# The causal mask of stick-breaking attention: from products on TensorE into VectorE's running sum

## The chip, the cores and the metric

The kernel runs on one core of one Trainium2 chip. The metric is the device time of one execution in microseconds; lower is better. The engines are named as the profile names them: PE is TensorE's matmul and PEld its weight load, DVE is VectorE, ACT is ScalarE, POOL is GpSimd, SP is SyncE, which issues most loads.

## The reference

One transformer block over 16 learned meta tokens and 512 tokens of width 1024: RMSNorm, one input projection for two attention branches of eight heads each, projections, gates, and a SwiGLU. The change lies in the first branch, stick-breaking attention:

```
z = jnp.einsum('bhqd,bhkd->bhqk', q, k).astype(jnp.float32) * (SB_HEAD_DIM ** -0.5)
causal = kpos[None, :] < qpos[:, None]
u = jnp.where(causal, jax.nn.log_sigmoid(-z), 0.0)
rest = lax.cumsum(u, axis=3, reverse=True) - u
log_a = jax.nn.log_sigmoid(z) + rest
a = jnp.where(causal, jnp.exp(log_a), 0.0)
return jnp.einsum('bhqk,bhkd->bhqd', a.astype(v.dtype), v)
```

A query sees only keys in front of it. With softplus(z) = max(z, 0) + ln(1 + exp(-|z|)), log_a is z minus the sum of softplus(z) over the visible keys from this one to the last visible one. The sum therefore runs from the last key back.

## The kernel before

Weights are split into a high and a low part (`split`, L78 on ACT, L79 on DVE), and each product is made of three matmuls (`mm3`, L290 to L292). Loads go through a ring of staging tiles from SP. Sums of weights for a seven-product scheme are made by accumulating DMAs that POOL issues (`tick`, L145), a few after each unit of work.

The main loop goes over eight stick-breaking heads and then eight differential heads. While a head's attention runs, PE does the projections of the next head ("units") between its stages: a head is a generator that yields how many units come before its next stage. The start of the program, up to the projections of head 0, is written in a fixed order for PE, DVE and ACT; from there a scheduler orders each engine's instructions by priority. In head 0 four further units (`sum_units`, L496 to L513) make sums of the activations (`f_t`, `tA`, `tB`) on DVE and ACT.

A stick-breaking head (`sb_head`) goes through these stages:

- Scores. Four blocks of 128 queries meet all keys up to their own (256, 272, 416 columns, and 528 in two halves). They lie in two PSUM tiles of two banks: `zA` holds blocks 0 to 2, `zB` block 3. Behind each block's three matmuls one more (L620) adds the mask: `ident_b`, a 128x128 identity in bfloat16, times `mask_b`, which holds -1e30 where key >= query and 0 elsewhere. It covers the 128 columns at the block's diagonal (144 for block 2).
- ACT takes Abs, Exp, Ln (L632 to L634), DVE makes softplus in `s` (L635).
- DVE sums `s` from the last key back, in place, with one scan per block (L639).
- DVE subtracts from the scores (L640), ACT takes the exponential (L641).
- `attn_out` transposes the weights on PE (L556, L568, L571), ACT and DVE split them (`a_h` L558, `a_l` L559), PE multiplies by the values (`vh`, `vl`, `vf`), and L659/L660 store the result. The values were transposed and split in `turn` (L532 to L540).

A masked score of about -1e30 has softplus 0, adds nothing to the sum, and its exponential is 0.

`mask_b` is made on POOL at the start (L1000, L1001), `ident_b` on DVE (L1004). A differential head makes a 128x528 table `bias` from `dist` on POOL (L700), in a single buffer of the pool `att`; DVE reads it with the scores (L711).

Of the kernel before, what the change touches and what calls it, by code (L numbers as in the profile page):

```python
# [9 lines left out]
F32 = mybir.dt.float32  # L10
F32R = mybir.dt.float32r
BF16 = mybir.dt.bfloat16
AF = mybir.ActivationFunctionType
ALU = mybir.AluOpType
AX = mybir.AxisListType

P = 128
D = 1024
SEQ = 512
NM = 16  # L20
L = NM + SEQ
KT = D // P
HL = L // 2
# [9 lines left out]
BIG = 1.0e30  # L33
# [8 lines left out]
def block_kernel(ctx: ExitStack, tc: tile.TileContext, x, meta, norm_mix_g, w_in, w_gate, b_gate,  # L42
                 lam_q1, lam_k1, lam_q2, lam_k2, subln_g, w_br_sb, w_br_df, w_out, norm_ffn_g,
                 w_ffn_gate, w_ffn_up, w_ffn_down, norm_final_g, out):
    nc = tc.nc
# [5 lines left out]
    const = ctx.enter_context(tc.tile_pool(name="const", bufs=1))  # L51
# [12 lines left out]
    def z_tile():  # L64
        return ps_z.tile([P, 2, 512], F32, tag="z", name="z")
# [221 lines left out]
    def mm3(ps, pairs, start=True, stop=True, skip=False):  # L287
        n = len(pairs)
        for i, (ah, al, bh, bl) in enumerate(pairs):
            nc.tensor.matmul(ps, lhsT=ah, rhs=bh, start=(start and i == 0), stop=False, skip_group_check=skip)  # L290
            nc.tensor.matmul(ps, lhsT=ah, rhs=bl, start=False, stop=False, skip_group_check=skip)  # L291
            nc.tensor.matmul(ps, lhsT=al, rhs=bh, start=False, stop=(stop and i == n - 1), skip_group_check=skip)  # L292
# [66 lines left out]
    ident = const.tile([P, P], F32, name="ident")  # L359
    make_identity(nc, ident)  # L360

    mask_b = const.tile([P, 144], BF16, name="mask_b")

    dist = const.tile([P, L], F32, name="dist")
    ident_b = const.tile([P, P], BF16, name="ident_b")
    ones_r = const.tile([P, P], F32R, name="ones_r")
    eps_t = const.tile([P, 1], F32, name="eps_t")
    pcol = const.tile([P, 33], F32, name="pcol")
# [27 lines left out]
    ap_ = att.enter_context(tc.tile_pool(name="att", bufs=1))  # L396
# [6 lines left out]

    a_s = ap_.tile([P, 256], F32, name="a_s")
    nc.gpsimd.memset(a_s, 0.0)

    def kv_units(key, evac):
        def unit(hf):
            s = slice(hf * HL, (hf + 1) * HL)
            ps = mm_tile()  # L410
            proj(ps[:, 0:HL], weights(key), xT, s)
            with tc.high_priority(offset=EVAC):
                evac(ps[:, 0:HL], s)

        return [lambda: unit(0), lambda: unit(1)]
# [195 lines left out]
    def sb_head(h, d, o_h, o_l):  # L611
        qh, ql = d["q"]
        kh, kl = d["k"]
        zA, zB = z_tile(), z_tile()

        def score(o, t, k0, k1, mo, mn):
            q = slice(t * P, (t + 1) * P)
            mm3(o, [(qh[:, q], ql[:, q], kh[:, k0:k1], kl[:, k0:k1])], stop=(mn == 0))
            if mn:
                nc.tensor.matmul(o[:, mo:mo + mn], lhsT=ident_b, rhs=mask_b[:, 0:mn], start=False, stop=True)  # L620

        score(zA[:, 0, 0:256], 0, 0, 256, NM, P)
        score(zA[:, 0, 144:416], 1, 0, 272, NM + P, P)
        score(zA[:, 1, 0:416], 2, 0, 416, NM + 2 * P, 144)
        score(zB[:, 0, 0:HL], 3, 0, HL, 0, 0)
        score(zB[:, 1, 0:HL], 3, HL, L, 400 - HL, P)
        res = []
        for z, n in ((zA, 416), (zB, HL)):
            zz = z[:, :, 0:n]
            e = ap_.tile([P, 2, n], F32, tag=("w2" if n == 416 else "w1"), name="e")  # L630
            s = ap_.tile([P, 2, n], F32, tag=("w3" if n == 416 else "w0"), name="s")
            nc.scalar.activation(e, zz, AF.Abs)  # L632
            nc.scalar.activation(e, e, AF.Exp, scale=-1.0)
            nc.scalar.activation(e, e, AF.Ln, bias=1.0)  # L634
            nc.vector.scalar_tensor_tensor(s, zz, 0.0, e, op0=ALU.max, op1=ALU.add)  # L635
            sf = s.rearrange("p a b -> p (a b)")
            for a, b in (((0, 144), (144, 416), (416, 832)) if n == 416 else ((0, L),)):
                f = sf[:, a:b][:, ::-1]
                nc.vector.tensor_tensor_scan(f, f, f, 0.0, op0=ALU.add, op1=ALU.bypass)  # L639
            nc.vector.tensor_tensor(s, zz, s, op=ALU.subtract)  # L640
            nc.scalar.activation(s, s, AF.Exp)  # L641
            res.append(sf)
        base = ((0, 0), (0, 144), (0, 416), (1, 0))
        zs = []

        def banks():
            if zs:
                return [z[:, 1] for z in zs]
            zs.extend((z_tile(), z_tile()))
            return [z[:, 0] for z in zs]  # L650

        t1, t2, av = attn_out(lambda t, k0, k1: res[base[t][0]][:, base[t][1] + k0:base[t][1] + k1], d, 96, banks)
        yield 4 if h + 1 < SEVEN else 5
        t1()
        yield 1
        t2()
        yield 1
        ps = av()
        nc.scalar.copy(o_h, ps)  # L659
        nc.vector.tensor_tensor(o_l, ps, o_h.bitcast(F32), op=ALU.subtract)  # L660
# [291 lines left out]
    zA, zB = z_tile(), z_tile()  # L952
# [33 lines left out]
    for k in range(KT):  # L986
# [10 lines left out]
    pm = mm_tile()  # L997
    nc.tensor.transpose(pm[:, 0:33], prow, ident[0:33, 0:33])
    nc.vector.tensor_copy(pcol[:, 8:33], pm[:, 8:33])
    nc.gpsimd.memset(mask_b, 0.0)  # L1000
    nc.gpsimd.affine_select(out=mask_b, in_=mask_b, pattern=[[-1, 144]], compare_op=ALU.is_gt,  # L1001
                            fill=-BIG, base=0, channel_multiplier=1)
    nc.vector.tensor_copy(ones_r, onesf)
    nc.vector.tensor_copy(ident_b, ident)  # L1004
    order.close()
    units[5]()
    turn()
    todo = []
    for br in range(2):
        name, head = (("y_sb", sb_head), ("y_df", df_head))[br]  # L1010
        if br:
            nc.gpsimd.memset(a_s, 0.0)
            y_out.append(xtp.tile([P, KT, SEQ], F32, tag="y_sb", name="y_out"))
        for h in range(NH):
# [5 lines left out]
            if h % 2 == 0:  # L1020
                o = [opool.tile([P, 2, SEQ], F32R, tag=t, name=t) for t in ("o_h", "o_l")]
# [513 lines left out]
```

## Time and profile before

| | |
|---|---|
| median of 3 runs | 954.66 us (953.51 to 954.71) |
| the profiled execution's own time | 955.27 us |
| its span | 953.5 us |
| mean granted TensorE clock | 0.998 |
| DMA, mean over the span | 166 GB/s |
| 32 mask products on PE (L620) | 230 ns each by the profile |
| 32 scans on DVE (L639) | 25.1 us busy |

The span runs from the first to the last instruction; the execution's own time has 1.8 us around it. Rows of the timeline give start, duration, engine, line, operation and what it writes and reads, then in brackets the idle time before it and what ended it. A PE row lasts until its result is out, and the next one starts long before that, so distances between starts tell what a matmul costs. The stick-breaking heads fill about 22 to 254 us, the differential heads the time to about 500 us.

### The profile page before, as it was taken

The page shows a single profiled execution, that of the slowest core. Times are in us where ns is not written, and L with a number is a line of the kernel's source. Part 1 is how long each engine was busy: PE and PEld are TensorE (multiplying, and loading weights), DVE is VectorE, ACT ScalarE, POOL GpSimd, SP SyncE. Part 2 cuts the span into 40 slices and gives each one's busy share as a digit, 9 for nine tenths or more (in the row PEclk, how much of TensorE's full clock was granted, in tenths as well). Part 3 has the DMA queues.
Part 4 walks back from the last instruction along what each step waited for, and adds up shares of the span by engine and source line. Part 5 has one row for each costly group of instructions (what it writes and reads, how often), then busy time and mean ns, then how long its engine had stood idle before and what let it go on. Part 6 is the DMA issues. An engine that isn't in the chain of part 4 may idle for free.

```text
span 953.5 us, 16249 instructions
## 1 busy us (share of the span) xinstructions
PE 940.6 (99%) x6105; PEld 851.1 (89%) x6106; DVE 720.8 (76%) x1336; ACT 592.8 (62%) x1137; POOL 190.5 (20%) x212
## 2 busy tenths in 40 slices
PE   8999999999999999999999999999999999999996
PEld 5988989898999899998987888899999999988886
DVE  7978777765677666876662578899888888989875
ACT  7765676666566666666676356765555555666654
POOL 3200121222133343344513530001000000000013
PEclk9999999999999999999999999999999999999999
DMA  8525678778777879799987865527743343276642
GB/s 246 154 63 149 164 176 204 159 166 228 198 178 174 213 170 185 181 204 180 199 198 168 260 197 170 150 78 171 155 123 111 90 120 103 67 255 203 198 151 89
DMA packets 155824, 158.42 MB, mean 166 GB/s; under 512 B 6465, under 2 KB 117218, under 8 KB 155746
## 3 DMA queue, kind: packets, MB, share of 16 engines
q1 hardware_dynamic: 132690, 101.61, 35.5%
q0 software_dynamic: 22896, 55.72, 28.6%
q8 instruction: 48, 0.79, 0.3%
q14 instruction: 30, 0.25, 0.1%
q10 hardware_dynamic: 160, 0.07, 0.0%
HBM read 133.64 MB, written 50.86 MB: 193 GB/s over the span
## 4 chain that ended last, share of the span: by engine, by line
PE 90%; DVE 6%; ACT 2%; issue 1%; DMA 1%; ACTq 0%; DVEq 0%
PE mm L290 21%; PE mm L291 21%; PE mm L292 21%; PE z L290 6%; PE z L291 6%; PE z L292 6%; PE z L708 1%; PE z L707 1%; DVE wl L79 1%; PE tr L556 1%; PE tr L532 1%; PE z L556 1%; DMA slots<-in_w_ffn_down_dram 1%; PE z L584 1%; DVE hres L1212 1%
## 5 line engine op out<-in xcount | busy, mean ns | idle before, releaser
L290 PE MATMUL mm<-xT_h,wh 128*128 128x264 f32 (+2 forms) x656 | 214.5, 327 | 0.5 <-ACT xT_h L912 0.5
L291 PE MATMUL mm<-xT_l,wh 128*128 128x264 f32 (+2 forms) x656 | 213.4, 325 | 0.5
L292 PE MATMUL mm<-xT_h,wl 128*128 128x264 f32 (+2 forms) x656 | 212.5, 324 | 0.0
L79 DVE TENSOR_TENSOR wl<-wst,wh 128x1024 fp32r<-128x1024 f32 (+1 forms) x147 | 164.2, 1120 | 44.9 <-ACT wh L78 44.7
L78 ACT CAST wh<-wst 128x1024 fp32r<-128x1024 f32 (+1 forms) x147 | 141.6, 965 | 84.7 <-PE mm L291 62.5
L291 PEld LDWEIGHTS mm<-xT_l,wh 128*128 128x128 f32 x656 | 123.5, 188 | 10.1 <-DVE xT_l L913 1.3
L290 PEld LDWEIGHTS mm<-xT_h,wh 128*128 128x128 f32 x656 | 123.5, 188 | 10.0 <-ACT xT_h L912 0.9
L292 PEld LDWEIGHTS mm<-xT_h,wl 128*128 128x128 f32 x656 | 123.4, 188 | 10.0
L290 PE MATMUL mm<-hT_h,wh 128*128 128x256 f32 x304 | 85.7, 284 | 0.4 <-ACT hT_h L1169 0.4
L292 PE MATMUL mm<-hT_h,wl 128*128 128x256 f32 x304 | 86.0, 284 | 0.0
L291 PE MATMUL mm<-hT_l,wh 128*128 128x256 f32 x304 | 86.0, 283 | 0.0
L290 PEld LDWEIGHTS mm<-hT_h,wh 128*128 128x128 f32 x304 | 57.3, 189 | 0.6 <-ACT hT_h L1169 0.6
L291 PEld LDWEIGHTS mm<-hT_l,wh 128*128 128x128 f32 x304 | 57.6, 190 | 0.0
L292 PEld LDWEIGHTS mm<-hT_h,wl 128*128 128x128 f32 x304 | 57.4, 189 | 0.0
L711 DVE CUSTOM_DVE_ANT_0 pr<-z,bias 128x144 f32<-128x144 f32 (+3 forms) x64 | 30.9, 501 | 35.0 <-PE z L708 34.9
L290 PE MATMUL mm<-o_h,wh 128*128 128x512 f32 x128 | 53.2, 416 | 0.0
L1437 POOL TENSOR_TENSOR outs<-hres,gF 128x512 f32<-128x512 f32 x4 | 6.2, 1554 | 226.0 <-DVE hres L1423 217.8
L291 PE MATMUL z<-wl,da 128*128 128x512 f32 (+1 forms) x132 | 50.4, 381 | 0.3 <-DVE wl L79 0.3
L145 POOL DMA_DIRECT2D ds<-in_w_ffn_down_dram x36 | 30.1, 840 | 102.3 <-ACT wh L78 68.6
L291 PE MATMUL mm<-o_l,wh 128*128 128x512 f32 x128 | 50.1, 392 | 0.3 <-DVE o_l L779 0.3
L290 PE MATMUL z<-wh,da 128*128 128x512 f32 (+1 forms) x132 | 50.2, 381 | 0.0
L292 PE MATMUL z<-wh,da 128*128 128x512 f32 (+1 forms) x132 | 50.2, 380 | 0.0
(375 smaller groups left out, 2554.4 us busy)
## 6 DMA issues: line engine op xcount, KB each, us to landing
wst<-in_w_in_dram SPq DMA_DIRECT2D x40, 512.0 KB, 5.7
ds<-in_w_ffn_down_dram POOLq DMA_DIRECT2D x30, 512.0 KB, 6.2
wst<-in_w_ffn_gate_dram SPq DMA_DIRECT2D x22, 512.0 KB, 4.0
wsu<-in_w_ffn_up_dram SPq DMA_DIRECT2D x20, 512.0 KB, 3.8
wst<-in_w_gate_dram SPq DMA_DIRECT2D x16, 512.0 KB, 6.8
y_df<-y_out POOLq DMA_DIRECT2D x32, 256.0 KB, 7.4
slots<-ds SPq DMA_DIRECT2D x13, 512.0 KB, 3.4
os<-in_w_out_dram POOLq DMA_DIRECT2D x12, 512.0 KB, 5.4
```

The source lines that it names most:

```text
L78: cast["last"] = (hi_copy or nc.scalar.copy)(hi, src)
L79: (lo_eng or nc.vector).tensor_tensor(lo, src, hi.bitcast(F32), op=ALU.subtract)
L145: tc.add_manual_dep(nc.gpsimd.dma_start(dst, src, **kw).ins, cast["last"].ins.name, paced)
L290: nc.tensor.matmul(ps, lhsT=ah, rhs=bh, start=(start and i == 0), stop=False, skip_group_check=skip)
L291: nc.tensor.matmul(ps, lhsT=ah, rhs=bl, start=False, stop=False, skip_group_check=skip)
L292: nc.tensor.matmul(ps, lhsT=al, rhs=bh, start=False, stop=(stop and i == n - 1), skip_group_check=skip)
L532: nc.tensor.transpose(pt[:, j * P:(j + 1) * P], vT[:, j * P:(j + 1) * P], ident)
L556: nc.tensor.transpose(pt[:, (t - j) * P:(t - j + 1) * P], blocks(t, j * P, (j + 1) * P), ident)
L584: nc.tensor.matmul(ps.rearrange("p (t q) -> p t q", q=P)[:, :, lo_rows:P], lhsT=vf[:, 1], rhs=a_s[:, 0:4 * qn], start=False, stop=True)
L707: nc.tensor.matmul(o, lhsT=q[c][:, qs], rhs=k[c][:, 0, k0:k1], start=True, stop=False)
L708: nc.tensor.matmul(o, lhsT=q[c][:, qs], rhs=k[c][:, 1, k0:k1], start=False, stop=True)
L711: nc.vector.tensor_tensor_reduce(po, zz, bb, scale=1.0, scalar=-3.0e38, op0=ALU.add, op1=ALU.max, accum_out=mx[:, t, c:c + 1])
```

## The change

The mask leaves the scores. Each scan now computes state = `resets` x state + `s`, from the last key back, and begins at 1e30. Over the keys behind the last visible one the state stays at about 1e30 (their softplus is lost in it), so their weights become exp(-1e30) = 0. `resets` is 1 except at one key per query, the last visible one, where it is 0: there the state falls to that key's own softplus, and the sum runs on from there. The table is 528 wide: ones, set by POOL, and 1 minus the identity in columns 399 to 526, made by DVE. A block of n columns reads the last n columns of it. It lies in the buffer that `bias` uses later (the pool `att` has one such buffer).

```
-    mask_b = const.tile([P, 144], BF16, name="mask_b")
-    ident_b = const.tile([P, P], BF16, name="ident_b")
+    resets = ap_.tile([P, L], F32, tag="bias", name="resets")
...
-        def score(o, t, k0, k1, mo, mn):
+        def score(o, t, k0, k1):
             q = slice(t * P, (t + 1) * P)
-            mm3(o, [(qh[:, q], ql[:, q], kh[:, k0:k1], kl[:, k0:k1])], stop=(mn == 0))
-            if mn:
-                nc.tensor.matmul(o[:, mo:mo + mn], lhsT=ident_b, rhs=mask_b[:, 0:mn], start=False, stop=True)
+            mm3(o, [(qh[:, q], ql[:, q], kh[:, k0:k1], kl[:, k0:k1])])
...
-            for a, b in (((0, 144), (144, 416), (416, 832)) if n == 416 else ((0, L),)):
+            for a, b in (((0, 144), (144, 416), (416, 816)) if n == 416 else ((0, L),)):
                 f = sf[:, a:b][:, ::-1]
-                nc.vector.tensor_tensor_scan(f, f, f, 0.0, op0=ALU.add, op1=ALU.bypass)
+                nc.vector.tensor_tensor_scan(f, resets[:, L - (b - a):][:, ::-1], f, BIG, op0=ALU.mult, op1=ALU.add)
...
-    nc.gpsimd.memset(mask_b, 0.0)
-    nc.gpsimd.affine_select(out=mask_b, in_=mask_b, pattern=[[-1, 144]], compare_op=ALU.is_gt,
-                            fill=-BIG, base=0, channel_multiplier=1)
+    nc.gpsimd.memset(resets, 1.0)
+    nc.vector.tensor_scalar(resets[:, 399:399 + P], ident, -1.0, 1.0, op0=ALU.mult, op1=ALU.add)
     nc.vector.tensor_copy(ones_r, onesf)
-    nc.vector.tensor_copy(ident_b, ident)
```

On PE, in the scores of head 1, this stands before (from the second block's last product on):

```order
L292 MATMUL z<-kh,ql 128x272
L620 LDWEIGHTS ident_b
L620 MATMUL z<-mask_b,ident_b 128x128
L290 MATMUL z<-kh,qh 128x416
L291 MATMUL z<-kl,qh 128x416
L292 MATMUL z<-kh,ql 128x416
L620 LDWEIGHTS ident_b
L620 MATMUL z<-mask_b,ident_b 128x144
L290 MATMUL z<-kh,qh 128x264
```

and this now (lines below the first edits are 3 to 5 lower in the changed kernel):

```order
L292 MATMUL z<-kh,ql 128x272
L290 MATMUL z<-kh,qh 128x416
L291 MATMUL z<-kl,qh 128x416
L292 MATMUL z<-kh,ql 128x416
L290 MATMUL z<-kh,qh 128x264
```

Four weight loads and four matmuls are gone from each head; in heads 1 to 7 nothing else on PE is moved. On DVE, in head 0, this stood between the last sum tile of the first two steps (`tB`) and the subtractions (the scans are shown as scalar_tensor_tensor on `s` alone):

```order
L501 SCALAR_TENSOR_TENSOR tB<-f_t_591,tB 128x528
L535 TENSOR_TENSOR vl<-tr,vh 128x384
L79 TENSOR_TENSOR wl<-wst,wh 128x1024
L496 TENSOR_TENSOR f_t_592<-xT_h,xT_l 128x528
L635 SCALAR_TENSOR_TENSOR s<-z,e 128x832
L496 TENSOR_TENSOR f_t_594<-xT_h,xT_l 128x528
L639 SCALAR_TENSOR_TENSOR s<-s 128x144
L639 SCALAR_TENSOR_TENSOR s<-s 128x272
L639 SCALAR_TENSOR_TENSOR s<-s 128x416
L635 SCALAR_TENSOR_TENSOR s<-z,e 128x528
L640 TENSOR_TENSOR s<-z,s 128x832
L639 SCALAR_TENSOR_TENSOR s<-s 128x528
```

and this stands there now:

```order
L534 TENSOR_TENSOR vl<-tr,vh 128x384
L500 SCALAR_TENSOR_TENSOR tB<-f_t_587,tB 128x528
L79 TENSOR_TENSOR wl<-wst,wh 128x1024
L495 TENSOR_TENSOR f_t_588<-xT_h,xT_l 128x528
L495 TENSOR_TENSOR f_t_590<-xT_h,xT_l 128x528
L632 SCALAR_TENSOR_TENSOR s<-z,e 128x832
L632 SCALAR_TENSOR_TENSOR s<-z,e 128x528
L636 SCALAR_TENSOR_TENSOR s<-resets,s 128x144
L636 SCALAR_TENSOR_TENSOR s<-resets,s 128x272
L636 SCALAR_TENSOR_TENSOR s<-resets,s 128x400
L636 SCALAR_TENSOR_TENSOR s<-resets,s 128x528
L637 TENSOR_TENSOR s<-z,s 128x832
```

`vl` and `tB` have changed places, the second `f_t` is ahead of the softplus steps, both softplus steps are ahead of the scans, and all four scans are ahead of the first subtraction. ACT's order moves with it in head 0: `vh` is cast before the small copy `v_s`, and Abs of the 528-column scores comes before Ln of the 832-column ones. On PE, in head 0 alone, the last two transposes of the second score turn (L556) stand two matmuls later, the third turn two, and the product with the values one.

On POOL the table of the first differential head stood near the start (`os` and `ds` are DMAs of the weight sums):

```order
L922 TENSOR_TENSOR wl<-wst,wh 128x1024
L996 MEMSET dist 64x64
L700 TENSOR_SCALAR bias<-dist 128x528
L145 DMA os_2_77<-in_w_out_dram 256x1x512
L145 DMA os_0_78<-in_w_out_dram 256x1x512
```

and stands now at the change of branches, in front of the DMAs that copy the keys of that head (`dk`):

```order
L145 DMA ds_8_94<-in_w_ffn_down_dram 256x1x512
L800 DMA y_sb_117<-ys 128x512
L697 TENSOR_SCALAR bias<-dist 128x528
L145 DMA ds_10_95<-in_w_ffn_down_dram 128x512
L687 DMA dk_2785<-dk_2785 64x1056
L687 DMA dk_2786<-dk_2786 64x1056
```

It waits there until the last scan of stick-breaking head 7 has read `resets`.

More of the change, by code (lines that the diff above doesn't have):

```diff
@@ L614, in sb_head @@
         zA, zB = z_tile(), z_tile()
-        def score(o, t, k0, k1, mo, mn):
+        def score(o, t, k0, k1):
             q = slice(t * P, (t + 1) * P)
-            mm3(o, [(qh[:, q], ql[:, q], kh[:, k0:k1], kl[:, k0:k1])], stop=(mn == 0))
-            if mn:
[L620 to L626, printed above, removed]
+            mm3(o, [(qh[:, q], ql[:, q], kh[:, k0:k1], kl[:, k0:k1])])
+        score(zA[:, 0, 0:256], 0, 0, 256)
+        score(zA[:, 0, 144:416], 1, 0, 272)
+        score(zA[:, 1, 0:416], 2, 0, 416)
+        score(zB[:, 0, 0:HL], 3, 0, HL)
+        score(zB[:, 1, 0:HL], 3, HL, L)
         res = []
```

## The prediction

> **What bounds the kernel now.** I read the page's busy line and its chain of work first, then the busy times by stage (each row of the windows: stretch, its length, then busy time and count of PE, PEld, DVE, ACT, POOL, the granted clock, the DMA share).
>
> ```profile
> PE 940.6 (99%) x6105; PEld 851.1 (89%) x6106; DVE 720.8 (76%) x1336; ACT 592.8 (62%) x1137; POOL 190.5 (20%) x212
> PE 90%; DVE 6%; ACT 2%; issue 1%; DMA 1%; ACTq 0%; DVEq 0%
> 22.00:57.00 35.00, 34.13 (x256) 32.08 (x256) 34.89 (x60) 23.93 (x47) 8.14 (x5) 1.00 0.38 106
> 85.00:113.00 28.00, 28.00 (x187) 25.13 (x184) 20.53 (x32) 17.17 (x33) 3.81 (x5) 1.00 0.56 149
> 197.00:225.00 28.00, 28.00 (x184) 25.17 (x185) 18.63 (x29) 18.55 (x36) 6.48 (x9) 1.00 0.73 157
> ```
>
> The chain is 90% PE. But a share over the whole run says little about this change, which touches only the eight stick-breaking heads. There the windows show two regimes. In heads 1 to 7 PE is busy 28.00 of 28.00 us at clock 1.00 while DVE has about 20 of 28. In head 0 (22 to 57 us) DVE is the full engine, 34.89 of 35.00. The chain of waits in order of time confirms it: one row per head for the score transposes, always at the same distance.
>
> ```profile
> 80.72 0.76 PE z L556 x7
> 108.68 0.77 PE z L556 x7
> ...
> 249.81 0.77 PE z L556 x7
> ```
>
> 108.68 − 80.72 = 27.96 us is a head's period, set by PE. What shortens PE's stream in heads 1 to 7 comes off the end; what shortens it in head 0 does so only as far as DVE lets it.
>
> **Term 1: the mask products in heads 1 to 7.** Removed are 32 matmuls, four a head, each with its own weight load. The profile gives 230 ns for one, but matmuls overlap, so the price is read from starts, not durations.
>
> ```profile
> L620 PE MATMUL z<-mask_b,ident_b x32: 229/230/237, 35.1 to 235.4; 128*128 128x128 bf16 x24, 128*128 128x144 bf16 x8
> 65.62 0.23 PE L620 MATMUL z<-mask_b,ident_b 128*128 128x128 bf16 x1
> 65.66 0.37 PE L290 MATMUL z<-kh,qh 128*128 128x272 f32 x1
> 65.86 0.29 PE L291 MATMUL z<-kl,qh 128*128 128x272 f32 x1
> 65.99 0.28 PE L292 MATMUL z<-kh,ql 128*128 128x272 f32 x1
> ...
> 67.30 0.28 PE L290 MATMUL z<-kh,qh 128*128 128x264 f32 x1
> 67.41 0.28 PE L291 MATMUL z<-kl,qh 128*128 128x264 f32 x1
> 67.54 0.28 PE L292 MATMUL z<-kh,ql 128*128 128x264 f32 x1
> 67.66 0.23 PE L620 MATMUL z<-mask_b,ident_b 128*128 128x128 bf16 x1
> 67.70 0.37 PE L290 MATMUL mm<-xT_h,wh 128*128 128x264 f32 x1
> 67.90 0.28 PE L291 MATMUL mm<-xT_l,wh 128*128 128x264 f32 x1
> 68.02 0.28 PE L292 MATMUL mm<-xT_h,wl 128*128 128x264 f32 x1
> ```
>
> From the first mask to the second matmul behind it: 65.86 − 65.62 = 0.24 us for mask and one 272-wide matmul; such a matmul alone takes 65.99 − 65.86 = 0.13. The mask cost 0.11 to 0.12. The last: 67.90 − 67.66 = 0.24, less 68.02 − 67.90 = 0.12 for a 264-wide one, is 0.12. The matmul right behind a mask is the slow one (0.20 start to start); without a mask in front, 67.30 to 67.41 where a new bank begins, it is 0.11. So both halves go. Four at 0.12 are 0.48 a head; seven heads: **−3.4 us**.
>
> DVE, ACT and POOL are idle a quarter of the time or more here, and nothing but PE must speed up for it. ACT's Abs of the first scores, which waited for the third mask, starts with them.
>
> **Term 2: the running sums.** Four scans a head stay. Before, both tensor operands were the score tile itself (add, then bypass); now one is `resets` (multiply, then add), from 1e30.
>
> ```profile
> L639 DVE TENSOR_TENSOR_SCAN s<-s 128x528 f32<-128x528 f32 x8 | 9.9, 1233 | 0.0
> L640 DVE TENSOR_TENSOR s<-z,s 128x528 f32<-128x528 f32 x8 | 5.6, 697 | 0.0
> L639 DVE TENSOR_TENSOR_SCAN s<-s 128x416 f32<-128x416 f32 x8 | 8.0, 998 | 0.0
> 72.86 3.13 DVE L639 TENSOR_TENSOR_SCAN s<-s 128x144 f32<-128x144 f32 x4
> 76.93 1.43 ACT L641 ACTIVATE s<-s 128x832 f32<-128x832 f32 x2 [1.29 <-DVE s L640]
> 80.56 0.92 PE L556 MATMUL z<-ident,s 128*128 128x128 f32 x7
> ```
>
> No row shows a scan with multiply and add. Between 416 and 528 columns it takes (1233 − 998)/112 = 2.1 ns a column. The ends I take are the plain tensor_tensor (697 ns, half the price, −1.5 us a head) and twice today's (+3.1 us a head). I take today's price: it is the same instruction, already with two streams, and that row is the nearest. The 400-column form saves 16 x 2.1 = 0.03 us. [...]
>
> If the scan is dearer, heads 1 to 7 hide some of it: the exponentials of head 1 end at 76.93 + 1.43 = 78.36, and PE takes the transposes at 80.56. That is 2.2 us, about 2.1 once a mask less lies between. Head 0 hides none.
>
> **Term 3: head 0.** Here PE waits for DVE.
>
> ```profile
> 53.02 0.28 PE L291 MATMUL mm<-xT_l,wh 128*128 128x264 f32 x1
> 54.04 0.44 PE L556 MATMUL z<-ident,s 128*128 128x128 f32 x2 [0.74 <-DVE a_l L559]
> 35.31 1.21 DVE L79 TENSOR_TENSOR wl<-wst,wh 128x1024 fp32r<-128x1024 f32 x1
> 36.53 1.04 DVE L501 SCALAR_TENSOR_TENSOR tB<-f_t,tB 128x528 fp32r<-128x528 f32 x1
> 37.49 0.54 DVE L535 TENSOR_TENSOR vl<-tr,vh 128x384 fp32r<-128x384 f32 x1
> 36.53 0.48 ACT L534 CAST vh<-tr 128x384 fp32r<-128x384 f32 x1
> 38.76 0.92 ACT L634 ACTIVATE e<-e 128x832 f32<-128x832 f32 x1
> 39.57 0.61 ACT L632 ACTIVATE e<-z 128x528 f32<-128x528 f32 x1
> 40.89 0.65 ACT L634 ACTIVATE e<-e 128x528 f32<-128x528 f32 x1
> 32.67 5.26 POOL L700 TENSOR_SCALAR bias<-dist 128x528 f32<-128x528 f32 x1
> ```
>
> Between 53.02 and 54.04 PE loses 1.02 − 0.12 = 0.9 us. Its 0.48 us from the masks of head 0 falls into that wait, so what counts is when DVE finishes `a_l`. In the new order:
> - `vl` stands before the last `tB`. DVE is free at 36.53; `vh`, one place earlier on ACT, is ready near 36.9. So DVE idles 0.35 us. But that `tB` took 1.04 us, while POOL's bias ran beside it, against 0.70 for its shape; the bias is no longer there. 0.35 lost, about 0.35 won: 0.
> - ACT now does Abs of the 528-column scores before the Ln of the 832: that Ln ends near 40.3, when DVE, with one `f_t` pulled ahead, arrives. Then DVE wants the other Ln, which ends at 40.89 + 0.65 = 41.54 as before; DVE has finished the 832-wide step near 41.3: 0.25 idle. This is the one real loss.
> - `resets` is made where `ident_b` was cast, at the same 128x128 size: 0.
> - On PE the two transposes that wait now stand two matmuls later, 2 x 0.12 = 0.24 us of work done before the wait instead of behind it.
>
> +0.25 − 0.03 − 0.24 is **0.0 us**. Bounds: −1.4 if DVE stopped limiting (0.9 wait and 0.48 masks), +0.4 if the idle times come out longer.
>
> **Term 4: the bias of the first differential head.** It shares the buffer of `resets` and must wait for the last scan of head 7.
>
> ```profile
> 239.93 3.13 DVE L639 TENSOR_TENSOR_SCAN s<-s 128x144 f32<-128x144 f32 x4
> 249.53 0.57 POOL L145 DMA_DIRECT2D ds<-in_w_ffn_down_dram  x1 [13.59 <-ACT wh L78]
> L711 DVE CUSTOM_DVE_ANT_0 pr<-z,bias x64: 301/496/708, 262.9 to 483.5; 128x144 f32<-128x144 f32 x16, 128x272 f32<-128x272 f32 x16, 128x400 f32<-128x400 f32 x16, 128x528 f32<-128x528 f32 x16
> ```
>
> It starts at 239.93 + 3.13 = 243.1 and at worst takes the 5.26 us of today: 248.3. Queued behind it on POOL are a weight-sum DMA, which waits for ACT until 249.53 anyway, and the two `dk` DMAs; its reader comes at 262.9. Cover of 1.2 and 14 us: 0. Were the cover gone, `dk` and with it head 0's scores would shift by the excess.
>
> **Sum.** −3.4 + 0 + 0 + 0 against the profiled execution's own 955.27 us is 951.9; that execution lies 0.6 above the median of 954.66, so the median becomes **951.3 us**.
>
> **Rivals.**
> - *The masks cost PE less than they seem.* If only the 0.04 us between a mask's start and the next start goes (65.62 to 65.66) and the slow start behind stays, 28 x 0.04 = 1.1: 953.5. Against it is the bank change at 67.30 without a slow start. [...] Chance 0.06, half for a price so low that it falls within 0.2%.
> - *The scan is dearer, but within the cover* (half again: 3.13/2 = +1.55 us): head 0 pays, heads 1 to 7 do not: 952.8. Chance 0.07.
> - *Slower.* At twice the price each of heads 1 to 7 waits 3.1 − 2.1 = 1.0 us at the transposes, 0.5 more than it saves, and head 0 pays 3.1: −3.4 + 3.1 + 7 x 1.0 = +6.7, 961.4. It turns positive from about +2.3 us a head. Chance 0.04.
> - *The saving does not reach the end:* the mask goes, but a weight DMA or DVE takes its place as the bound in heads 1 to 7: 954.7. Against it: PE never waits there, and at 197 to 225 us the DMA share is 0.73. Chance 0.07.
> - *Head 0 shortens too* (a cheaper scan, or none of the idle times): 949.9. Chance 0.06.
>
> **How the numbers follow.** The forecast has 0.70. A measurement of this kernel can tell about 0.2% (1.9 us) from no change. The forecast, the shorter head 0 and half of the first rival lie beyond that: faster 0.70 + 0.06 + 0.03 = 0.79; slower 0.04; the rest 0.17. The range, 949.7 to 953.5, takes in the bounds of head 0, the dearer scan within its cover and the cheaper masks; the unreached end and the slower case are left out.
>
> **What would show it.** Right: no row of the mask; the distance of the L556 rows of heads 1 to 7 down from 27.96 to about 27.48; scans of 1233 and 697-like lengths unchanged; PE's wait before the two transposes near 54 us still there and about as long or longer; POOL's bias between 243 and 249 us with nobody waiting. Wrong: a scan over 1.3 us at 528 columns; an idle PE before L556 in heads 1 to 7; the period unchanged.

## The result, and the profile after

The changed kernel takes 947.55 us (median of 5 runs, 947.32 to 949.43); the kernel before took 954.61 beside it (5 runs, 953.51 to 954.71). The ratio is 0.9932, 95% interval 0.9921 to 0.9944. So 7.1 us went, where the prediction had 3.4. The time is faster, as forecast, but lies 2.2 us below the range.

The page's busy line and its chain of work, and three stretches of the windows, for the changed kernel:

```profile
PE 933.7 (99%) x6073; PEld 846.4 (89%) x6074; DVE 719.2 (76%) x1336; ACT 589.8 (62%) x1137; POOL 186.4 (20%) x211
PE 86%; DVE 7%; ACT 4%; issue 2%; DMA 1%; ACTq 0%; DVEq 0%
22.00:57.00 35.00, 33.82 (x249) 31.54 (x250) 34.42 (x57) 23.96 (x47) 3.13 (x4) 1.00 0.38 106
85.00:113.00 28.00, 28.00 (x182) 25.42 (x183) 21.02 (x32) 17.46 (x36) 4.04 (x5) 1.00 0.56 147
197.00:225.00 28.00, 28.00 (x183) 25.43 (x182) 19.09 (x30) 18.83 (x36) 6.15 (x8) 1.00 0.75 170
```

PE still bounds the kernel, at the same clock (0.999 by the profiled run, 0.998 before). The 32 mask products are gone. The period of a head is read, as before, from the score transposes in the chain of waits:

```profile
80.55 0.76 PE z L555 x7
107.99 0.77 PE z L555 x7
...
135.44 0.76 PE z L555 x7
163.24 0.77 PE z L555 x7
...
218.13 0.76 PE z L555 x7
246.96 0.77 PE z L555 x7
```

107.99 − 80.55 = 27.44 us against 27.96: 0.52 a head, where 0.48 was forecast. From 218.13 to 246.96 it is 28.83, where the kernel before had 29.33 (220.48 to 249.81). From 135.44 to 163.24 it is 27.80: head 4 has a new hesitation of PE. The timeline shows it, and beside it the work of ACT that it follows:

```profile
152.65 0.41 ACT L445 COPY qq<-mm 128x264 f32<-128x264 f32 x1
...
152.74 0.28 PE L292 MATMUL mm<-xT_h,wl 128*128 128x264 f32 x1
153.11 0.39 PE L290 MATMUL mm<-tA,wh 128*128 128x264 f32 x1
```

0.37 us from start to start where 0.12 is usual. The matmul starts when ACT has copied a finished product out of PSUM: `qq` ends at 152.65 + 0.41 = 153.06. A hesitation of 0.2 us also stands in e9's profile, told below, and none in those of e1 and e10. In the kernel before, which has none either, the same copy ends at 153.62 + 0.37 = 153.99, 0.56 us ahead of that matmul (154.55).

The scans by shape, with busy time and mean duration in ns:

```profile
L636 DVE TENSOR_TENSOR_SCAN s<-resets,s 128x528 f32<-128x528 f32 x8 | 9.9, 1232 | 0.0
...
L637 DVE TENSOR_TENSOR s<-z,s 128x528 f32<-128x528 f32 x8 | 5.6, 700 | 0.0
L636 DVE TENSOR_TENSOR_SCAN s<-resets,s 128x400 f32<-128x400 f32 x8 | 7.7, 966 | 0.0
```

1232 ns against 1233: a scan with multiply, add and a second tile to read costs what the one with add and bypass did. The 400-column form saves 998 − 966 = 0.03 us.

So the heads give what was forecast, and something else gave as much again. To find where, the start of the same matmul was taken from both traces, all along the span (mask products left out of the count), and the time before subtracted from the time after. The rows of the table are such places, named by their time in the kernel before; the other columns are experiments told below.

| place, us in before | after | e1 | e4 | e9 | e10 |
|---|---|---|---|---|---|
| 34.8, in head 0 | +0.3 | −0.6 | +0.2 | +0.6 | −0.1 |
| 65.5, scores of head 1 | +0.3 | −0.5 | +0.2 | +0.7 | 0.0 |
| 235.4, scores of head 7 | −2.8 | −3.8 | +0.2 | −2.5 | −3.2 |
| 646.6, FFN products begin | −3.2 | −3.5 | −0.1 | −1.6 | −3.3 |
| 830.4, near their end | −6.1 | −3.5 | −3.5 | −1.6 | −6.3 |
| 953.5, end of the span | −6.6 | −3.8 | −3.3 | −2.4 | −6.9 |

Between 65.5 and 235.4 us, with all masks of heads 1 to 7, 3.1 us go. Between 646.6 and 830.4 us another 2.9 go, in a stage that the change does not touch: same instructions, same order on PE. The windows of that stage, before and then after:

```profile
642.00:832.00 190.00, 190.00 (x1595) 190.00 (x1594) 164.15 (x257) 105.67 (x174) 5.33 (x7) 1.00 0.45 120
700.00:720.00 20.00, 20.00 (x169) 20.00 (x169) 16.82 (x27) 10.99 (x19) 0.00 (x0) 1.00 0.36 106
```

```profile
642.00:832.00 190.00, 189.53 (x1612) 188.89 (x1611) 166.27 (x260) 107.23 (x177) 5.26 (x6) 1.00 0.45 119
700.00:720.00 20.00, 20.00 (x173) 20.00 (x172) 16.22 (x27) 10.46 (x17) 0.00 (x0) 1.00 0.34 99
```

PE is never idle there before and the clock is 1.00 in both, yet 173 matmuls fit in 20 us where 169 did. It is not a wait that went: each matmul takes less room. Which ones, the timeline of PE shows, before:

```profile
699.84 0.28 PE L291 MATMUL mm<-t_l,wh 128*128 128x256 f32 x1
...
700.78 0.28 PE L290 MATMUL z<-hT_h,wh 128*128 128x256 f32 x1
...
701.99 0.28 PE L291 MATMUL z<-hT_l,wh 128*128 128x256 f32 x1
```

and after:

```profile
699.80 0.28 PE L290 MATMUL z<-t_h,wh 128*128 128x256 f32 x1
...
700.82 0.28 PE L290 MATMUL mm<-hT_h,wh 128*128 128x256 f32 x1
...
702.00 0.28 PE L291 MATMUL mm<-hT_l,wh 128*128 128x256 f32 x1
```

Before, 8 matmuls on the sums of activations (`t`) take 0.94 us, 117 ns each; after, 9 take 1.02, 113 ns each. The 10 on the activations themselves (`hT`) that follow take 1.21 and 1.18 us, 121 and 118 ns each. The 717 matmuls of 256 columns on `t` tiles, nearly all of them in this stage, went from a mean of 118.6 ns start to start to 114.4: 717 x 4.2 ns = 3.0 us. Those on `hT` went from 119.9 to 119.4, some 0.5 us more, and PE now idles 0.5 us in the stage (189.53 of 190 busy). This stage holds 2.9 us of what was not forecast, which is 6.6 − 3.4 = 3.2 us between these two traces and 3.7 by the medians.

### The profile page after: what moved, and what is told of

Same layout as the page of the kernel before. It is cut to its first block, busy times and chain, and to the rows that moved or that the text cites. A ratio compares the mean times of both kernels' runs of the same rounds, so it can differ in the third digit from the quotient of the medians.

```text
span 946.9 us, 16184 instructions
## 1 busy us (share of the span) xinstructions
PE 933.7 (99%) x6073; PEld 846.4 (89%) x6074; DVE 719.2 (76%) x1336; ACT 589.8 (62%) x1137; POOL 186.4 (20%) x211
## 4 chain that ended last, share of the span: by engine, by line
PE 86%; DVE 7%; ACT 4%; issue 2%; DMA 1%; ACTq 0%; DVEq 0%
PE mm L290 20%; PE mm L291 20%; PE mm L292 20%; PE z L290 6%; PE z L291 6%; PE z L292 6%; DVE wl L79 2%; PE z L705 1%; PE z L704 1%; DMA wsu<-in_w_ffn_up_dram 1%; ACT wh L78 1%; PE tr L555 1%; PE tr L531 1%; PE z L555 1%; DVE hres L1207 1%
## 5 line engine op out<-in xcount | busy, mean ns | idle before, releaser
L292 PE MATMUL mm<-o_h,wl 128*128 128x512 f32 x128 | 50.1, 391 | 0.0
```

## The experiments

What could make the same matmul shorter? In the compiled programs one thing differs in that stage: addresses. `mask_b` (288 bytes a partition) and `ident_b` (256) lay in the pool `const`, below everything else in SBUF. Without them the weights `wh`, `wl` and all that follows lie 544 bytes lower, while the `t` sums, allocated from the right end, stay where they were. Take as the **offset** the address of the weights that the next matmul loads, minus the address of the data that the running matmul moves, modulo 256 bytes. For `t_h` it was 32832 − 204768, modulo 256 = 96; now it is 32288 − 204768, modulo 256 = 64. For `hT` it is 0 in both kernels.

The theory (placement): the offset sets the pitch of these matmuls. The rivals: the work taken out frees the stage in some other way, or the time hangs on something else in the program.

**e1: the work gone, the old placement.** In the changed kernel, ahead of `dist`:

```
+    const.tile([P, 136], F32, name="pad_c")
```

> The changed kernel with one unused tile of 544 bytes a partition put back into the constant pool, where the mask and its identity lay before. All instructions and their order stay; every tile behind it in SBUF lies 544 bytes higher, as in the kernel before, while the t sums of the feed-forward part (allocated from the other side) stay where they are. Theory A (a matmul's pitch depends on where its moving tile and the next weights lie against each other): the 256-column products of the t tiles in the feed-forward part go back from about 114 ns to about 118.5 ns start to start, and about 3 of the 7 us are lost: 950.5 us. Theory B (the second half of the gain comes from work removed, from DMA or from the order): nothing changes, 947.5 us.

**e2: padding that leaves the offset at 64.** 512 is twice 256, so weights and `t` sums keep their offset.

```
+    const.tile([P, 128], F32, name="pad_c")
```

> The same with an unused tile of 512 instead of 544 bytes. In the two traces the pitch of 256-column products sorts by one number, the address of the next weights minus that of the moving data, modulo 128 bytes: 64 gives 114 ns, 0 about 119.5, 96 about 118.6. Theory A with this rule: 512 bytes leave that number as in the changed kernel (64), so 947.5 us although almost the whole shift is back. Theory A without the rule (the old region of addresses is slower): 950.5 us. Theory B: 947.5 us.

**e3: 64 bytes of padding**, which make the offset of `t` 128.

```
+    const.tile([P, 16], F32, name="pad_c")
```

> The same with an unused tile of 64 bytes. The number for the t products becomes 0 modulo 128. Theory A with the rule: those 764 and more matmuls of 256 columns go from 114 to about 119.5 ns, 1000 x 5 ns = 4 to 5 us more than the changed kernel: 951.5 us. Without the rule (a shift of 64 bytes is almost nothing): 947.5 us. Theory B: 947.5 us.

**e4: the old work, the new placement.** In the kernel before, both tiles go to the pool `att`, behind the weights:

```
-    mask_b = const.tile([P, 144], BF16, name="mask_b")
-    ident_b = const.tile([P, P], BF16, name="ident_b")
...
+    mask_b = ap_.tile([P, 144], BF16, name="mask_b")
+    ident_b = ap_.tile([P, P], BF16, name="ident_b")
     v_s = ap_.tile([P, P], F32, name="v_s")
```

> The kernel before, with its mask products, but the two mask tiles taken from the attention pool instead of the constant pool, so that all tiles between them lie 544 bytes lower, as in the changed kernel. Theory A: the feed-forward part gains its 3 us without any change of work: 951.5 us against 954.6. Theory B: 954.6 us, no change.

Measured, beside 954.75 us of before (13 runs, 953.80 to 955.77):

| | us, median (range, runs) | ratio to before (95%) | offset of `t` | pitch on `t`, ns |
|---|---|---|---|---|
| e1, 544 bytes | 951.74 (951.48 to 952.21, 7) | 0.9970 (0.9959 to 0.9981) | 96 | 118.6 |
| e2, 512 bytes | 947.60 (947.42 to 949.05, 5) | 0.9933 (0.9920 to 0.9945) | 64 | 114.4 |
| e3, 64 bytes | 951.46 (950.54 to 952.48, 5) | 0.9967 (0.9955 to 0.9980) | 128 | 118.9 |
| e4, masks moved | 951.71 (951.39 to 952.10, 7) | 0.9970 (0.9958 to 0.9981) | 64 | 114.4 |

The windows of the FFN stage, first e1, then e4:

```profile
642.00:832.00 190.00, 190.00 (x1595) 190.00 (x1593) 163.94 (x255) 106.82 (x176) 5.28 (x6) 1.00 0.44 116
```

```profile
642.00:832.00 190.00, 189.93 (x1622) 189.73 (x1621) 167.07 (x262) 107.18 (x178) 5.30 (x7) 1.00 0.45 120
```

All four went as the placement theory said, though e1 lies 1.2 us above its forecast. e1 has the changed work and the count of matmuls of the kernel before; e4 has the old work and more matmuls in the stretch. Unused padding of 544 or 64 bytes takes the extra gain away, and 512 bytes leave it. The two parts separate: the work alone is worth 3.0 us in the old placement (954.75 − 951.74), the placement alone 3.0 us with the old work (954.75 − 951.71). Both together gave 7.1, 1.1 more than the sum. The intervals of these ratios are about 1 us to each side, so the difference may be noise; nothing here explains it.

**e9: only the `t` sums moved.** Does it take the distance, or would any shift of 544 bytes do? In the changed kernel the padding stands above the `t` sums alone, so that they lie 544 bytes lower and nothing else does:

```
     tsum = {n: tuple(tp.tile([P, 4, 256], F32R, name=f"{n}_{c}") for c in "hl") for n in ("t1", "t2", "t4")}
+    tp.tile([P, 136], F32, name="pad_t")
```

> The changed kernel with 544 bytes a partition of padding above the t sums alone, so that they lie 544 bytes lower and everything else stays where the changed kernel has it. Theory (the distance between the next weights and the moving data sets the pitch of the FFN's 256-column products): 951.0, between 950.5 and 951.7 as with the padding ahead of everything else (e1), and the products that move the t sums back at 118.6 ns. Rival (the 544 bytes counted elsewhere, through some other tile or an absolute address): 947.5 and 114.4 ns.

```profile
642.00:832.00 190.00, 190.00 (x1594) 190.00 (x1593) 163.84 (x256) 106.42 (x175) 5.28 (x6) 1.00 0.45 117
```

952.50 us (10 runs, 951.06 to 953.69; before 954.89; ratio 0.9973, 0.9964 to 0.9983). The offset is 96 again and so is the pitch: 118.6 ns, on tiles at other addresses than in any run so far. The FFN stage gains 0.0 in the table above. The median is 0.8 above the forecast range: in its profiled run PE also waited once for DVE's split of weights, 0.71 us near 539 us, in a part that the padding does not touch. That is named, not explained.

**e5: the same offset for `hT`.** If 64 is good for `t`, it should be for the 1136 matmuls on `hT`, whose offset is 0. Their tile has 16 spare columns in front; the edit uses the columns from 0 on:

```
-    hT_h, hT_l = (xtp.tile([P, NM + KT * SEQ], F32R, tag=t, name=n)[:, NM:].rearrange("p (k t) -> p k t", t=SEQ)
+    hT_h, hT_l = (xtp.tile([P, NM + KT * SEQ], F32R, tag=t, name=n)[:, 0:KT * SEQ].rearrange("p (k t) -> p k t", t=SEQ)
```

> The changed kernel with the normalized activations hT placed 64 bytes lower in their own tiles (the first 4096 columns of the tile instead of the last), so that weights minus hT is 64 modulo 128 bytes instead of 0. Same instructions, same order. Rule of the 128 bytes: some 1200 products of 256 columns fall from about 119.3 to 114.5 ns, 6 us: 941.5 us. If the rule held for the t tiles alone: 947.5 us.

945.72 us (6 runs, 943.26 to 949.28; before 954.85, 23 runs; ratio 0.9905, 0.9888 to 0.9923). That is the lowest median of all, but only 1.8 us under the changed kernel (947.55 − 945.72) where 6 were expected; as the intervals of the two ratios still touch (this one reaches 0.9923, the changed kernel's begins at 0.9921), a gain over the changed kernel is likely and not shown. The stage in two parts, the changed kernel first, then e5, and behind it e5's longest wait of PE in this stage:

```profile
642.00:720.00 78.00, 78.00 (x668) 78.00 (x667) 67.30 (x106) 43.08 (x70) 5.26 (x6) 1.00 0.59 141
720.00:832.00 112.00, 111.53 (x946) 110.89 (x946) 98.97 (x156) 64.15 (x107) 0.00 (x0) 1.00 0.35 103
```

```profile
642.00:720.00 78.00, 78.00 (x664) 78.00 (x664) 67.45 (x105) 43.77 (x71) 5.26 (x6) 1.00 0.59 140
720.00:832.00 112.00, 110.92 (x969) 110.12 (x968) 101.30 (x159) 64.75 (x108) 0.00 (x0) 1.00 0.36 109
...
PE mm L290 <- ACT qx L1317: 0.9, 1, 0.9
```

In the second part 23 more matmuls fit, in the first none. Over all, the pitch on `hT` fell to 115.7 ns and that on `t` rose to 115.3, and PE came upon a wait of 0.9 us for ACT that it had hardly had (0.3). But these means hide two states, which e5's timeline shows:

```profile
719.33 0.28 PE L290 MATMUL mm<-t_h,wh 128*128 128x256 f32 x1
...
721.10 0.28 PE L290 MATMUL z<-t_h,wh 128*128 128x256 f32 x1
...
721.33 0.28 PE L292 MATMUL z<-t_h,wl 128*128 128x256 f32 x1
721.58 0.39 PE L290 MATMUL mm<-hT_h,wh 128*128 128x256 f32 x1
721.80 0.28 PE L291 MATMUL mm<-hT_l,wh 128*128 128x256 f32 x1
...
722.03 0.28 PE L290 MATMUL mm<-hT_h,wh 128*128 128x256 f32 x1
...
723.73 0.28 PE L290 MATMUL mm<-hT_h,wh 128*128 128x256 f32 x1
```

From 719.33 to 721.10 it is 15 matmuls at 118 ns. Then PE stops for about 0.2 us in all (0.25 and 0.22 us from start to start, where 0.12 is usual), and from 722.03 to 723.73 it is 15 matmuls at 113. All of them, on `t` and on `hT`, have offset 64, 256 columns and 128 columns of weights. On both tiles the pitch is about 118 ns from the start of the stage up to the stop and about 113 behind it. So with this offset the fast pitch is possible but not certain. The change came with a stop; whether the stop made it, and how, is not shown.

**e6: 64 bytes more in front of the activations.** This moves `xT`, `hT` and all behind them and leaves weights and `t` sums in place, so the offsets of the 512-column products change too.

```
-    xtp.tile([P, 48], F32, name="pad_x")
+    xtp.tile([P, 64], F32, name="pad_x")
```

> The changed kernel with the small padding tile ahead of xT enlarged from 192 to 256 bytes. xT, hT, the outputs o, the merged mg and the token sums da move by 64 bytes against the weights, so that their number becomes 64 modulo 128; the t tiles keep theirs. hT alone gives 941.5 us as in the run before. The 512-column products (1550 of them at 227 ns, number 0): if the rule holds for them too, some 5 ns each, 7 us more: 934 us; if a longer stream covers the weight load anyway: 941.5 us; if 64 is wrong for them, above 942 us.

953.32 us (12 runs, 950.57 to 954.93; ratio 0.9980, 0.9971 to 0.9989): the last of its cases. Modulo 256 the products did not all come to 64. Of those with 512 columns, which stood at offset 0 and 227.7 ns in the changed kernel, some 510 that load activations as their weights came to 64 and 233.3 ns, and some 1,100 that move activations came to 192 and 229.5. The products on `hT` came to 192 as well, and to 117.7 ns. The windows under e8 show the first kind. The trace is of e6's fastest run (950.57); why the median lies 2.8 us higher it can't show.

**e7: an offset of 32 for `hT`**, with `[:, NM // 2:NM // 2 + KT * SEQ]` in the line of e5.

> The changed kernel with hT 32 bytes lower: weights minus hT is 32 modulo 128. Only the pitch of the hT products is of interest. If the two reads collide in 64-byte halves of a line, 32 lies between 0 (119.3 ns) and 64 (114.5 ns), like 96 (118.6 ns): 117 to 119 ns, 945.5 to 947.5 us. If only the exact 0 is bad: 114.5 ns, 941.5 us.

950.46 us (one run): a miss. The pitch on `hT` came to 118.3 ns, but that on `t` rose to 117.7 though its offset had not changed. The rise is the same on `t1`, `t2` and `t4` (117.6 to 117.9). So, as in e5, the offset of one pair does not settle the pitch; something else counts besides, and what was not found. That two reads collide, as the expectation supposes, no run shows.

**e8: the resets in a buffer of their own**, so that `bias` is not tied to the last scan. To make room, `pad_x` shrank by 128 bytes.

```
-    xtp.tile([P, 48], F32, name="pad_x")
+    xtp.tile([P, 16], F32, name="pad_x")
...
-    resets = ap_.tile([P, L], F32, tag="bias", name="resets")
+    resets = ap_.tile([P, L], F32, name="resets")
```

> The changed kernel with a buffer of its own for resets instead of the one of bias (the padding ahead of xT is 128 bytes smaller to make room, which keeps every number modulo 128). On POOL the bias of the first differential head goes back to its early place; nothing else moves. The prediction put this move at zero at the change of branches and at 0.35 us of DVE time in head 0, which a wait used up. That theory: within 0.4 us of the changed kernel, 947.5 to 948.0 us, with the last tB of the first sums stretched again beside POOL's bias. Rival (the late bias delays the first differential head): faster, below 947 us.

955.82 us (11 runs, 954.98 to 956.67; ratio 1.0011, 1.0002 to 1.0019): 8 us slower than the changed kernel, a plain miss. The down projection, 512 columns at a time, in the changed kernel, in e8 and in e6:

```profile
860.00:925.00 65.00, 65.00 (x288) 53.84 (x287) 54.28 (x75) 40.09 (x62) 5.02 (x3) 1.00 0.56 176
```

```profile
860.00:925.00 65.00, 65.00 (x281) 52.70 (x280) 54.24 (x75) 38.73 (x59) 3.62 (x2) 1.00 0.60 191
```

```profile
860.00:925.00 65.00, 65.00 (x280) 52.47 (x279) 52.66 (x71) 38.45 (x58) 3.63 (x2) 1.00 0.54 172
```

65 us / 288 = 225.7 ns a matmul, against 231.3 and 232.1. The shift of 128 bytes had put the 512-column products from offset 0 to 128. The expectation had supposed that 128 bytes make no difference. Over the program some 1,530 of them went from 227.7 to 232.3 ns, 7 of the 8 us.

**e10: the same buffer, with every offset kept.** Room comes from smaller constants, so that everything behind them lies 64 bytes lower, and 16 floats above the `t` sums put these 64 lower too.

```
-    resets = ap_.tile([P, L], F32, tag="bias", name="resets")
+    resets = ap_.tile([P, L], F32, name="resets")
...
-    cn = const.tile([P, 16], F32, name="cn")[:, 0:2]
+    cn = const.tile([P, 8], F32, name="cn")[:, 0:2]
...
-    eps_c = const.tile([P, 1], F32, name="eps_c")
-    var_max = const.tile([P, 1], F32, name="var_max")
+    ev = const.tile([P, 2], F32, name="ev")
+    eps_c, var_max = ev[:, 0:1], ev[:, 1:2]
...
+    tp.tile([P, 16], F32, name="pad_t")
```

> The changed kernel with the resets in a buffer of their own, so POOL makes the first differential bias early as before the change; room is made so that everything behind the constants lies 64 bytes lower, the t sums too, and every distance between weights and moving data stays as in the changed kernel. Theory (the miss of e8 was placement; the buffer itself costs nothing, an early bias stretches one DVE step of head 0 by 0.35 us): 947.5 to 948.1. Rival (sharing the buffer is itself worth the 8 us of e8): 955.8.

948.39 us (4 runs, 948.22 to 949.75; ratio 0.9935, 0.9919 to 0.9952): 0.3 above its forecast and 0.8 above the changed kernel, whose interval it overlaps. The buffer costs or brings nothing that can be told from noise here, and the 8 us of e8 were placement. All addresses differ from the changed kernel's, the offsets do not, and the pitches are its own: 114.4 ns on `t`, 119 to 120 on `hT`, 227 to 229 at 512 columns.

## Why the prediction was wrong

- **Term 1, the masks of heads 1 to 7 (−3.4): right.** 3.1 us went by the trace of the changed kernel between the scores of head 1 and of head 7, and 3.3, 3.2 and 3.1 in e1, e9 and e10. 3.2 / 28 = 0.11 us a mask, as read from starts, where the sum took 0.12. In the changed kernel the hesitation in head 4, where PE came to wait for ACT, took back 0.25 us of it; "nothing but PE must speed up" did not hold there. The scores of head 1 now follow each other without the slow start behind a mask:

```profile
65.82 0.28 PE L292 MATMUL z<-kh,ql 128*128 128x256 f32 x1
65.94 0.29 PE L290 MATMUL z<-kh,qh 128*128 128x272 f32 x1
66.06 0.29 PE L291 MATMUL z<-kl,qh 128*128 128x272 f32 x1
```

  The second matmul of 272 columns stands 0.12 us behind the first, where it stood 0.20 behind it. No run shows a mask price between 0.04 and 0.11 us, on which half of the first rival's chance (the 0.03 counted to faster) rests: the runs say 3.1 to 3.3 us for 28 masks, 0.11 to 0.12 us each.
- **Term 2, the scans (0): right**, 1232 ns against 1233. Today's price was the author's estimate, taken from the nearest row. A scan still takes 2.1 ns a column, from (1232 − 966)/128, and the plain subtraction 1.0, from 999 ns at 832 columns and 700 at 528; why a scan costs twice as much is not shown.
- **Term 3, head 0 (0.0, at most +0.4): right in size.** From 34.8 to 65.5 us it costs 0.0 to 0.1 in the changed kernel, e1, e9 and e10. Here is DVE's `a_l` before, and then DVE's rows and PE's wait after:

```profile
53.31 0.68 DVE L559 TENSOR_TENSOR a_l<-z,a_h 128x512 fp32r<-128x512 f32 x1
```

```profile
37.26 0.56 DVE L534 TENSOR_TENSOR vl<-tr,vh 128x384 fp32r<-128x384 f32 x1 [0.47 <-ACT vh L533]
37.73 0.70 DVE L500 SCALAR_TENSOR_TENSOR tB<-f_t,tB 128x528 fp32r<-128x528 f32 x1
...
40.72 1.77 DVE L632 SCALAR_TENSOR_TENSOR s<-z,e 128x832 f32<-128x832 f32 x2
42.41 3.09 DVE L636 TENSOR_TENSOR_SCAN s<-resets,s 128x144 f32<-128x144 f32 x4
...
53.92 0.68 DVE L558 TENSOR_TENSOR a_l<-z,a_h 128x512 fp32r<-128x512 f32 x1
```

```profile
53.35 0.28 PE L290 MATMUL mm<-xT_h,wh 128*128 128x264 f32 x1
54.66 0.44 PE L555 MATMUL z<-ident,s 128*128 128x128 f32 x2 [1.03 <-DVE a_l L558]
```

  `vl` waits 0.47 us (0.35 was forecast) and `tB` takes 0.70 as forecast. The 0.25 us of idle time between the two softplus steps, "the one real loss", hardly shows: both take 1.77 us together, against 1.02 and 0.68 before. `a_l` comes 0.6 later than before (53.92 against 53.31), of which 0.3 is the start of the program, where profiles differ anyway: that shift is −0.6 to +0.6 in the table. PE waits longer, 1.03 against 0.74, and of what it used to do behind the wait, two matmuls are done ahead of it. One reason of this term fell: `tB` was said to have taken 1.04 because POOL's bias ran beside it. But in the kernel before an earlier `tB` (33.45 us) ran wholly beside that bias and took 0.69; and in e10, where the bias again runs from 32.5 to 37.8 us, `tB` takes 0.70 from 37.3 on. Why it took 1.04 stays open.
- **Term 4, the bias behind head 7's last scan (0): right.** It starts 2.7 us before the forecast 243.1 and takes far less than the 5.26 us allowed for; the DMA behind it waits for ACT as before:

```profile
240.45 1.55 POOL L697 TENSOR_SCALAR bias<-dist 128x528 f32<-128x528 f32 x1 [6.86 <-DVE s L636]
246.74 0.62 POOL L145 DMA_DIRECT2D ds<-in_w_ffn_down_dram  x1 [4.74 <-ACT wh L78]
```

- **The step that failed is the sum.** "−3.4 + 0 + 0 + 0" counts the instructions that the change removes, adds and moves, and holds everything else equal. It has no term for the 544 bytes that the two constants leave free. With the placement of before, the same work measures 951.74 (e1), 0.4 from the predicted 951.3 and inside the range. The missing term is 717 matmuls x 4.2 ns = 3.0 us, in a stage that the prediction never looked at. None of the rivals had it; the nearest in time, a shorter head 0 at 949.9, was not what happened. That the freed bytes made the kernel faster and not slower was luck: other small shifts, of 64 bytes (e3) and of 128 (e8), cost 4 and 8 us against the changed kernel.

## What to carry to other kernels

A change that frees or takes bytes in SBUF moves the tiles allocated behind them (here the weights from 32832 to 32288); where PE is the bound, compare the pitch of untouched matmuls in an untouched stage before putting a gain down to the edit, and repeat the edit with padding that restores the addresses (e1) and the old kernel with the new addresses (e4). When room must be made for an experiment, keep the distances between weights and moving data modulo 256 bytes (e10: 948.39 us), or placement hides what is tested (e8: 955.82 us with the same buffer). Padding is itself a thing to tune: in this kernel it is worth as much as the edit (3.0 us each, e4 and e1).

## What the runs showed of the hardware

The pitch of FP32R matmuls here depends on where their operands lie. Mean start-to-start times over all twelve traces, by the offset defined above (matmuls of heads 1 and later, followed by one of the same width, 128 columns of weights; long gaps and offsets seen in fewer than 200 matmuls left out):

| offset, bytes | 256 columns, ns (count) | 512 columns, ns (count) |
|---|---|---|
| 0 | 119.5 (9885) | 227.8 (15254) |
| 32 | 118.3 (1137) | |
| 64 | 115.0 (6930) | 233.2 (529) |
| 96 | 118.6 (2154) | |
| 128 | 118.8 (2097) | 232.4 (1678) |
| 160 | | 234.3 (286) |
| 192 | 116.8 (1605) | 230.1 (1871) |

The two widths want different offsets: 64 has the lowest mean for 256 columns and is among the worst for 512, where 0 is the best. The 115.0 is a mean of two states: about 114 ns in most traces, about 118 in e7 and in the first part of e5. Products of 264 columns showed no clear effect, about 121 ns. Each step is 2 to 4%, but a kernel with thousands of such matmuls feels it: 3 us and 7 us here. e1, e4, e9 and e10 (118.6, 114.4, 118.6 and 114.4 ns) show that for the `t` products it is the distance and not the addresses themselves, and in all eight traces with `hT` at offset 0 the pitch on `t` followed its own offset (64: 114.4, 96: 118.6, 128: 118.9). But e5 shows that the offset alone does not fix it: the pitch was 118 ns up to a stop of 0.2 us and 113 behind it. What in the chip does it was not found.

POOL's bias, the same instruction on the same data, took 5.26 us at 33 us in the kernel before and 1.54 to 1.85 us in all eight heads of the changed kernel. DVE was busy beside it both at 33 us (sums of SBUF tiles) and at 240 us (steps that read the PSUM tiles `z` and `mm`). These rows do not tell the reason.
